# One core of Trainium2: attention values with the attention weights as the stationary operand, and a causal mask made by 64-row products

## The chip, the cores and the metric

The kernel runs on one core of one Trainium2 chip. The metric is the device time in microseconds (us) of one execution. TensorE (PE) does the matrix products and has a second row of records for its weight loads (PEld); VectorE (DVE), ScalarE (ACT) and GpSimd (POOL) do the rest; SyncE (SP) issues most transfers.

## The reference

One layer of an encoder runs for a prompt of 1024 tokens and a sample of 64 tokens. Only the second of its three head groups, the stick-breaking attention with 4 heads of 64, is touched:

```python
def sb_block(q, q_pos, k, v, k_pos):
    z = jnp.einsum('bqhd,bkhd->bhqk', q, k).astype(F32) * (B_HEAD_DIM ** -0.5)
    mask = (k_pos[None, :] < q_pos[:, None])[None, None]
    log_1m = jnp.where(mask, jax.nn.log_sigmoid(-z), 0.0)
    after = lax.cumsum(log_1m, axis=3, reverse=True) - log_1m
    w = jnp.where(mask, jnp.exp(jax.nn.log_sigmoid(z) + after), 0.0)
    return jnp.einsum('bhqk,bkhd->bqhd', w.astype(v.dtype), v)
...
    b_out = o_b.reshape(bsz, L, B_WIDTH) * jax.nn.silu(bg)
```

## The kernel before, in words

The whole layer is one program. Its stages follow each other along the span: norms and memory keys and values, the input projection with the HGRN2 scan beside it (to about 441 us), the attention beside the last projections (about 441 to 577 us), the output projection, cross-attention, and its output projection. Large products are split into three passes of high and low parts (`mm<-hhi,whi`, `mm<-hlo,whi`, `mm<-hhi,wlo`): they are the bulk of PE's work. Here they are called the main products.

The attention is `sb_all`. Two heads form a pair; a pair's keys lie on partitions 0 to 63 for one head and 64 to 127 for the other. A token tile is 128 queries (the ninth is the sample's 64). For each pair and tile there are one or two units, each of at most 512 keys; a tile of two units does the later keys first. That makes 13 units for a pair and 26 in all, of which 18 are a tile's first. A unit passes three steps:

- `scores` (line 629): for each head three products of queries and keys, 64 rows deep, into a bank `hg` each; the two heads' products alternate and use different halves of the array's rows. In a tile's first unit, a product of `identb` (identity) and `negmask` (128 rows deep) then adds -1e30 above the diagonal. ACT makes two sigmoids of each bank, DVE a scan and a product; the result is `sm`, a row for each query.
- `weights_T` (line 658): the weights are transposed on PE in blocks of 128 (`tp<-ident,sm`), and ACT copies them to `wT`, a row for each key.
- `values` (line 677): for each chunk of 128 keys and each head one product with the values `vb` as the stationary operand (128 rows, 64 columns) and `wT` as the moving one (128 queries). The heads fill different halves of the output's partitions. After the tile's last unit DVE multiplies the bank with the gate in `C`.

A product of plain float32 operands leaves two records on PE and two on PEld; a transpose leaves one of each, and so do the main products. The 148 products of values are 296 records.

Two layers set the order. A planner (`Sched`) runs each stage as a task and, at each `yield`, resumes the first task whose inputs it holds ready by its own table of costs; `sb_all` yields once per iteration `k`, which does `scores` of unit k, `values` of unit k-2 and `weights_T` of unit k-1. Then the tile framework orders the instructions of each engine once more by its own model, which can put an instruction of one step inside another. Banks are few: three `hg`, two `tp`, three `mm`.

Of the kernel before, what the change touches and what calls it, by code (L numbers as in the profile page):

```python
# [8 lines left out]
F32 = mybir.dt.float32  # L9
F32R = mybir.dt.float32r  # L10
BF16 = mybir.dt.bfloat16
# [4 lines left out]
P = 128  # L16
# [3 lines left out]
SMP = 64  # L20
# [18 lines left out]
def _rows(i):  # L39
    return P if i < 8 else SMP  # L40
# [64 lines left out]
def hybrid_step(  # L105
# [44 lines left out]
    def ps_tp():  # L150
        return ps.tile([P, 512], F32, tag="tp", name="tp", bufs=2)
# [33 lines left out]
    def tt(out, a, b, op):  # L185
        sch.op("DVE", 0.07 + free(out) / 960.0)
        cur['DVE'] = DVE.tensor_tensor(out=out, in0=a, in1=b, op=op)  # L187
# [20 lines left out]
    with tc.high_priority(offset=10 * URGENT):  # L208
        ones = const([P, P], F32, "ones")
        DVE.memset(ones, 1.0)  # L210
        ident = const([P, P], F32, "ident")
        make_identity(nc, ident)
        mhalf = const([P, 4], F32, "mhalf")
        POOL.memset(mhalf, -0.5)

        identb = const([P, P], BF16, "identb")
        negmask = const([P, P], BF16, "negmask")
        DVE.memset(negmask, 0.0)
        POOL.affine_select(out=negmask, in_=negmask, pattern=[[-1, P]], compare_op=ALU.is_gt,
                           fill=NEG, base=0, channel_multiplier=1)  # L220
        cur["masks"] = (identb, negmask)
        blkmask = const([P, 4], F32, "blkmask")
        DVE.memset(blkmask, 0.0)
        for i in range(4):
            DVE.memset(blkmask[32 * i:32 * i + 32, i:i + 1], 1.0)
        invw = const([P, 2], F32, "invw")
        invcnt = const([P, 2, 16], F32, "invcnt")
        for ct in range(2):
            POOL.iota(invcnt[:, ct, :], pattern=[[1, 16]], base=1, channel_multiplier=0,
                      allow_small_or_imprecise_dtypes=True)  # L230
            for g in range(2):
                w = float(2 << (2 * ct + g))
                rs = slice(64 * g, 64 * g + 64)
                DVE.memset(invw[rs, ct:ct + 1], 1.0 / w)

    def late_constants(pool):
        wpl = pool([P, 2, P], F32, "wpl")
        DVE.memset(wpl, 0.0)
        DVE.tensor_copy(identb, ident)
        for ct in range(2):  # L240
            for g in range(2):
                rs = slice(64 * g, 64 * g + 64)
                DVE.tensor_scalar(out=invcnt[rs, ct, :], in0=invcnt[rs, ct, :], scalar1=float(2 << (2 * ct + g)),
                                  scalar2=None, op0=ALU.min)
        DVE.reciprocal(invcnt, invcnt)
        for g in range(4):
            rs = slice(64 * (g % 2), 64 * (g % 2) + 64)
            POOL.dma_start(wpl[rs, g // 2, rs], w_pool[0, g])
        onorm = const([P, 4], F32, "onorm")
        POOL.dma_start(onorm, hgrn_onorm_g)  # L250
        pscale = const([P, 2], F32, "pscale")
        POOL.dma_start(pscale, pool_scale)
        cur["hgrn"] = (blkmask, onorm)
        cur["pool"] = (invw, invcnt, wpl, pscale)
# [359 lines left out]
    def sb_all(ops, pool):  # L614

        units = []
        for pair in range(2):
            for i in range(NT):
                base, W = (0, P * (i + 1)) if i < 8 else (SEQ, P + SMP)
                nkt = (W + P - 1) // P  # L620
                lo = 0 if W <= 512 else P * (nkt // 2)
                ps_ = [(lo, W)] if lo == 0 else [(lo, W), (0, lo)]
                for pi, (s0, s1) in enumerate(ps_):
                    units.append(dict(pair=pair, i=i, base=base, s0=s0, n=s1 - s0, first=pi == 0,
                                      last=pi == len(ps_) - 1, prev=[None, None]))
        for a, b in zip(units[:-1], units[1:]):
            b["before"] = a

        def scores(u):
            (qh, ql), (kh, kl), vb, cv = ops[u["pair"]]  # L630
            i, n, nq = u["i"], u["n"], _rows(u["i"])
            u["s"], u["m"] = [], []
            zs = [ps_hg(), ps_hg()]
            qs = slice(i * P, i * P + nq)
            ks = slice(u["base"] + u["s0"], u["base"] + u["s0"] + n)
            for pi, (q, k) in enumerate(((qh, kh), (qh, kl), (ql, kh))):
                for e in range(2):
                    own = slice(64 * e, 64 * e + 64)
                    mm(zs[e][:nq, :n], q[own, qs], k[own, ks], pi == 0, pi == 2 and not u["first"])
            if u["first"]:  # L640
                for z in zs:
                    mm(z[:nq, n - nq:n], cur["masks"][0][:nq, :nq], cur["masks"][1][:nq, :nq], False, True)
            for e, z in enumerate(zs):
                s = pool([P, 512], F32, "sm", 7)
                m = pool([P, 512], F32, "sm", 7)
                act(m[:nq, :n], z[:nq, :n], AF.Sigmoid, scale=-0.125)
                act(s[:nq, :n], z[:nq, :n], AF.Sigmoid, scale=0.125)
                p = None if u["first"] else u["before"]["m"][e]
                sch.op("DVE", 0.07 + n / 480.0)
                DVE.tensor_tensor_scan(m[:nq, :n][:, ::-1], m[:nq, :n][:, ::-1], m[:nq, :n][:, ::-1],  # L650
                                       1.0 if p is None else p[:nq, 0:1], ALU.mult, ALU.min)
                if p is not None:
                    tt(s[:nq, n - 1:n], s[:nq, n - 1:n], p[:nq, 0:1], ALU.mult)
                tt(s[:nq, :n - 1], s[:nq, :n - 1], m[:nq, 1:n], ALU.mult)
                u["s"].append(s)
                u["m"].append(m)

        def weights_T(u):
            i, n, nq = u["i"], u["n"], _rows(u["i"])
            npc = (n + P - 1) // P  # L660
            u["wT"] = []
            for e in range(2):
                s = u["s"][e]
                pt = ps_tp()
                wT = pool([P, 4, P], F32, "wT", 4)
                for c in range(npc):
                    w = min(P, n - c * P)
                    tr(pt[:w, c * P:c * P + nq], s[:nq, c * P:c * P + w], nq)
                ptv = pt.rearrange("p (c t) -> p c t", t=P)
                if i < 8:  # L670
                    act(wT[:, :npc, :], ptv[:, :npc, :], AF.Copy)
                else:
                    act(wT[:, 0, :nq], ptv[:, 0, :nq], AF.Copy)
                    act(wT[:SMP, 1, :nq], ptv[:SMP, 1, :nq], AF.Copy)
                u["wT"].append(wT)

        def values(u):
            (qh, ql), (kh, kl), vb, cv = ops[u["pair"]]
            i, n, nq = u["i"], u["n"], _rows(u["i"])
            npc = (n + P - 1) // P  # L680
            po = ps_hg() if u["first"] else u["before"]["po"]
            u["po"] = po
            for c in range(npc):
                for e in range(2):
                    own = slice(64 * e, 64 * e + 64)
                    first, last = u["first"] and c == 0, u["last"] and c == npc - 1
                    if i < 8:
                        mm(po[own, :nq], vb[:, u["s0"] // P + c, own], u["wT"][e][:, c, :], first, last, 0.147)
                    elif c == 0:
                        mm(po[own, :nq], cv[:, own], u["wT"][e][:, 0, :nq], first, last, 0.1)  # L690
                    else:
                        mm(po[own, :nq], vb[:SMP, 8, own], u["wT"][e][:SMP, 1, :nq], first, last, 0.1)
            if u["last"]:
                cs = C[:, i, 4 + u["pair"], :nq]
                tt(cs, po[:, :nq], cs, ALU.mult)
                sch.done[("sb", u["pair"], i)] = sch.t["DVE"]

        nu = len(units)
        for k in range(nu + 2):
            if k < nu:  # L700
                j, c = units[k]["pair"], units[k]["i"] // 3
                if units[k]["first"] and (k == 0 or units[k]["i"] % 3 == 0 or c == 2):
                    yield f"bv{j}{c}"
                ready = dict(sch.cur.dep)
                scores(units[k])
            if 0 <= k - 2 < nu:
                values(units[k - 2])
            if 0 <= k - 1 < nu:
                weights_T(units[k - 1])
            yield None  # L710


# [747 lines left out]
```

## Time and profile before

| | |
|---|---|
| median of 3 runs | 935.03 us (934.71 to 935.86) |
| the profiled execution | 935.02 us; its span 933.3 us, granted clock 0.996 |
| PE busy in the span | 914.2 us (98%) |
| PEld, DVE, ACT, POOL busy | 853.6, 556.6, 479.5, 107.2 us |

Busy time of PE is the union of its records. A record lasts some 270 ns although the next can start 110 ns after it, so how long a stretch of products takes is read from the starts of its first and of the next group. "Idle before" is what no record covers, and the releaser behind the arrow is what ended it. In a timeline the columns are the start, the time covered, and the group with its count.

### The profile page before, as it was taken

The numbers are of one execution on the slowest core, as the hardware profiler recorded it, in microseconds if no ns is written. First come the engines' busy times: TensorE is split into PE (matmuls) and PEld (weight loads), VectorE is DVE, ScalarE is ACT, GpSimd is POOL, SyncE is SP. The second block draws the span as 40 slices with busy tenths as digits, with TensorE's granted clock in tenths as the row PEclk, the third lists the DMA queues.
The fourth block names the chain that finished last, engine by engine and source line by source line (L and its number), as shares of the span: only waits on it lengthen the run. The fifth ranks groups of instructions, "written<-read, shape, count | busy, mean of one in ns | idle before, by whom it ended". The sixth has DMA issues, their size and how long they took to land.

```text
span 933.3 us, 18372 instructions
## 1 busy us (share of the span) xinstructions
PE 914.2 (98%) x7504; PEld 853.6 (91%) x7504; DVE 556.6 (60%) x1125; ACT 479.5 (51%) x1005; POOL 107.2 (11%) x194
## 2 busy tenths in 40 slices
PE   8899999999999999999999999999999999999997
PEld 7899999999998999989779788999999999999997
DVE  6849483674678574552684777565564545563343
ACT  7623384658767774963673765433452333342231
POOL 5502430010010010000000000211200000001110
PEclk9999999999999999999999999999999999999999
DMA  8815511011100111012111411222433111232231
GB/s 306 259 38 181 142 46 47 25 49 29 47 27 31 47 33 46 25 47 79 47 31 36 157 61 69 90 68 80 164 119 92 30 39 46 76 106 91 91 101 58
DMA packets 33126, 73.60 MB, mean 79 GB/s; under 512 B 5601, under 2 KB 18065, under 8 KB 33042
## 3 DMA queue, kind: packets, MB, share of 16 engines
q1 hardware_dynamic: 30112, 68.07, 22.7%
q0 software_dynamic: 1888, 4.35, 1.3%
q8 instruction: 59, 0.97, 0.4%
q14 instruction: 25, 0.20, 0.1%
q10 hardware_dynamic: 1042, 0.01, 0.1%
HBM read 56.45 MB, written 15.89 MB: 78 GB/s over the span
## 4 chain that ended last, share of the span: by engine, by line
PE 82%; DVE 6%; ACT 4%; DMA 4%; issue 2%; POOL 1%; DVEq 0%; POOLq 0%; ACTq 0%
PE mm L171 64%; PE hg L171 14%; PE tp L175 5%; DVE sm L650 3%; DVE sm L187 1%; DVE wlo L187 1%; ACT L183 1%; ACT whi L183 1%; DMA xt<-in_x_prompt_dram 1%; DVE hlo L187 1%; DMA wraw<-in_w_xk_dram 1%; DMA mkd<-mraw 1%; DMA wraw<-in_w_xo_dram 1%; DMA gT<-in_norm_mem_dram 1%; DMA mvd<-mtm 1%
## 5 line engine op out<-in xcount | busy, mean ns | idle before, releaser
L171 PE MATMUL mm<-hhi,whi 128*128 128x384 f32 (+2 forms) x1272 | 425.1, 334 | 0.0
L171 PE MATMUL mm<-hlo,whi 128*128 128x384 f32 (+2 forms) x1272 | 412.5, 325 | 0.0
L171 PE MATMUL mm<-hhi,wlo 128*128 128x384 f32 (+2 forms) x1248 | 405.3, 325 | 0.0
L171 PEld LDWEIGHTS mm<-hhi,whi 128*128 128x128 f32 x1272 | 239.2, 188 | 6.3 <-issue 1.3
L171 PEld LDWEIGHTS mm<-hlo,whi 128*128 128x128 f32 x1272 | 239.5, 188 | 1.2 <-issue 0.9
L171 PEld LDWEIGHTS mm<-hhi,wlo 128*128 128x128 f32 x1248 | 234.6, 188 | 0.4 <-issue 0.3
L187 DVE TENSOR_TENSOR wlo<-wraw,whi 128x1024 fp32r<-128x1024 f32 (+1 forms) x53 | 63.5, 1200 | 56.6 <-ACT whi L183 56.3
L183 ACT ACT_TABLE_LOAD x66 | 84.7, 1283 | 19.0 <-DVE E L187 12.0
L183 ACT ACTIVATE whi<-wraw 128x1024 fp32r<-128x1024 f32 (+1 forms) x53 | 55.3, 1043 | 71.5 <-PE mm L171 54.7
L183 ACT ACTIVATE wraw<-mm 128x384 f32<-128x384 f32 (+3 forms) x51 | 22.9, 449 | 72.8 <-PE mm L171 62.9
L650 DVE TENSOR_TENSOR_SCAN sm<-sm 128x384 f32<-128x384 f32 (+4 forms) x52 | 48.3, 938 | 14.0 <-ACT sm L183 14.0
L183 ACT ACTIVATE sm<-hg 128x384 f32<-128x384 f32 (+4 forms) x104 | 42.2, 485 | 15.7 <-PE hg L171 8.7
L187 DVE TENSOR_TENSOR wraw<-mm,gain 128x384 f32<-128x384 f32 (+1 forms) x48 | 24.4, 510 | 41.6 <-ACT wraw L183 41.3
L1241 POOL TENSOR_TENSOR small<-small 128x1 f32<-128x1 f32 (+1 forms) x18 | 4.2, 234 | 375.3 <-ACT wraw L183 375.3
L183 ACT ACTIVATE E<-E 128x512 f32<-128x512 f32 (+1 forms) x68 | 32.8, 515 | 10.5 <-DVE E L187 9.9
L171 PE MATMUL mm<-mhi,wlo 128*128 128x256 f32 x128 | 35.8, 289 | 1.8 <-DVE wlo L187 1.8
L321 POOL TENSOR_TENSOR small<-small,mhalf 128x1 f32<-128x1 f32 (+2 forms) x50 | 36.0, 719 | 4.2
L171 PE MATMUL mm<-mhi,whi 128*128 128x256 f32 x128 | 36.2, 293 | 0.1
L171 PE MATMUL mm<-mlo,whi 128*128 128x256 f32 x128 | 35.1, 283 | 0.0
L443 POOL COPY qf<-q 128x512 f32<-128x512 f32 (+1 forms) x12 | 14.6, 1218 | 177.6 <-PE hg L171 140.7
L187 DVE TENSOR_TENSOR wlo<-C,whi 128x1024 fp32r<-128x1024 f32 x16 | 19.6, 1225 | 24.9 <-ACT whi L183 23.4
L191 DVE SCALAR_TENSOR_TENSOR C<-wraw,small,C 128x384 f32<-128x384 f32 (+3 forms) x54 | 27.8, 569 | 10.2 <-POOL small L321 10.2
(209 smaller groups left out, 1409.1 us busy)
## 6 DMA issues: line engine op xcount, KB each, us to landing
wraw<-in_w_in_dram SPq DMA_DIRECT2D x28, 512.0 KB, 3.6
xt<-in_x_prompt_dram SPq DMA_DIRECT2D x8, 512.0 KB, 6.5
wraw<-in_w_xv_dram SPq DMA_DIRECT2D x8, 512.0 KB, 3.9
wraw<-in_w_out_dram SPq DMA_DIRECT2D x8, 512.0 KB, 3.6
C<-in_x_prompt_dram SPq DMA_DIRECT2D x8, 512.0 KB, 3.5
x1d<-C SPq DMA_DIRECT2D x8, 512.0 KB, 2.8
wraw<-in_w_xq_dram SPq DMA_DIRECT2D x8, 512.0 KB, 3.6
wraw<-in_w_xo_dram SPq DMA_DIRECT2D x8, 512.0 KB, 3.6
```

The source lines that it names most:

```text
L171: cur['PE'] = PE.matmul(out, lhsT=lhsT, rhs=rhs, start=start, stop=stop, skip_group_check=True)
L175: PE.transpose(out, in_, ident[:n, :n])
L183: cur['ACT'] = ACT.activation(out, in_, func, **kw)
L187: cur['DVE'] = DVE.tensor_tensor(out=out, in0=a, in1=b, op=op)
L191: DVE.scalar_tensor_tensor(out=out, in0=a, scalar=s, in1=b, op0=op0, op1=op1)
L321: POOL.tensor_tensor(out=r[:n, :w], in0=r[:n, :w], in1=mhalf[:n, :w], op=ALU.pow)
L443: POOL.tensor_copy(qf[:, 1, :], qq)
L650: DVE.tensor_tensor_scan(m[:nq, :n][:, ::-1], m[:nq, :n][:, ::-1], m[:nq, :n][:, ::-1], 1.0 if p is None else p[:nq, 0:1], ALU.mult, ALU.min)
L1241: POOL.tensor_tensor(out=ms[:n, 0:1], in0=ms[:n, 0:1], in1=ms[:n, pi:pi + 1], op=ALU.add)
```

## The change

The values' product changes sides: `wT` (128 queries wide) becomes the stationary operand and `vb` (64 columns of one head) the moving one. The output has a row for each query; the heads lie side by side in columns of the bank. The first and the second unit of a tile write different 128 columns, since each closes its own sum. After the tile's last unit ACT copies the bank to `vo`, DVE adds the second half where there is one, and a new step `gated`, one iteration later, transposes `vo` on PE and multiplies with the gate. The iteration now does `scores` of unit k, `weights_T` of k-1, `gated` of k-3, `values` of k-2. The mask is made of products 64 rows deep and 64 columns wide: `picks` holds identity blocks for each half of the rows, and two products for each head replace the one. The planner's cost of a product of values goes from 0.147 (0.1 for the sample's) to 0.113.

```diff
-        identb = const([P, P], BF16, "identb")
-        negmask = const([P, P], BF16, "negmask")
+        picks = const([P, 2, P], BF16, "picks")
+        negmask = const([P, 64], BF16, "negmask")
...
+        for e in range(2):
+            POOL.affine_select(out=negmask[64 * e:64 * e + 64], in_=negmask[64 * e:64 * e + 64], pattern=[[-1, 64]],
+                               compare_op=ALU.is_gt, fill=NEG, base=0, channel_multiplier=1)
...
-        DVE.tensor_copy(identb, ident)
+        DVE.memset(picks, 0.0)
+        for e in range(2):
+            es = slice(64 * e, 64 * e + 64)
+            for i in range(2):
+                DVE.tensor_copy(picks[es, i, 64 * i:64 * i + 64], ident[es, es])
+            DVE.memset(picks[64 * e:64 * e + 1, 1, 0:64], 1.0)
...
             if u["first"]:
-                for z in zs:
-                    mm(z[:nq, n - nq:n], cur["masks"][0][:nq, :nq], cur["masks"][1][:nq, :nq], False, True)
+                picks, negmask = cur["masks"]
+                for hf in range(nq // 64):
+                    for e in range(2):
+                        own = slice(64 * e, 64 * e + 64)
+                        c0 = n - nq + 64 * hf
+                        mm(zs[e][:nq, c0:c0 + 64], picks[own, hf, :nq], negmask[own], False, hf == nq // 64 - 1)
...
-            for c in range(npc):
-                for e in range(2):
-                    own = slice(64 * e, 64 * e + 64)
-                    first, last = u["first"] and c == 0, u["last"] and c == npc - 1
-                    if i < 8:
-                        mm(po[own, :nq], vb[:, u["s0"] // P + c, own], u["wT"][e][:, c, :], first, last, 0.147)
...
+            c0 = 0 if u["first"] else P
+            for e in range(2):
+                own = slice(64 * e, 64 * e + 64)
+                for c in range(npc):
+                    kn = SMP if i == 8 and c else P
+                    v = cv if i == 8 and c == 0 else vb[:, 8 if i == 8 else u["s0"] // P + c]
+                    mm(po[:nq, c0 + 64 * e:c0 + 64 * e + 64], u["wT"][e][:kn, c, :nq], v[:kn, own], c == 0, c == npc - 1,
+                       0.113)
             if u["last"]:
+                vo = pool([P, P], F32, "vo", 1)
+                act(vo[:nq], po[:nq, :P], AF.Copy)
+                if c0:
+                    tt(vo[:nq], po[:nq, P:2 * P], vo[:nq], ALU.add)
+                u["vo"] = vo
+
+        def gated(u):
+            i, nq = u["i"], _rows(u["i"])
+            if u["last"]:
+                pt = ps_tp()
+                tr(pt[:, :nq], u["vo"][:nq], nq)
                 cs = C[:, i, 4 + u["pair"], :nq]
-                tt(cs, po[:, :nq], cs, ALU.mult)
+                tt(cs, pt[:, :nq], cs, ALU.mult)
...
+            if 0 <= k - 1 < nu:
+                weights_T(units[k - 1])
+            if 0 <= k - 3 < nu:
+                gated(units[k - 3])
             if 0 <= k - 2 < nu:
                 values(units[k - 2])
-            if 0 <= k - 1 < nu:
-                weights_T(units[k - 1])
```

The order of PE's instructions in the two programs shows what becomes of a unit. (A product's two records are one row here; the size is that of its output.) This is the first unit of the last prompt tile of the second pair before: scores and mask, then the values of the unit two before it, then the transposes of the one just before it.

```order
L171 MATMUL hg<-kh,qh 128x512 x2
L171 MATMUL hg<-kl,qh 128x512 x2
L171 MATMUL hg<-kh,ql 128x512 x2
L171 LDWEIGHTS identb
L171 MATMUL hg<-negmask,identb 128x128
L171 LDWEIGHTS identb
L171 MATMUL hg<-negmask,identb 128x128
L171 MATMUL hg<-wT,vb 64x128 x8
L175 MATMUL tp<-ident,sm 128x128 x6
```

The same place on PE after the change, from the last of the four mask products on, with the tile's second unit behind it:

```order
L171 MATMUL hg<-negmask,picks 128x64
L175 MATMUL tp<-ident,sm 128x128 x6
L171 MATMUL hg<-vb,wT 128x64 x8
L171 MATMUL hg<-kh,qh 128x512
L171 MATMUL hg<-kl,qh 128x512
L171 MATMUL hg<-kh,qh 128x512
L171 MATMUL hg<-kl,qh 128x512
L175 MATMUL tp<-ident,vo 128x128
L171 MATMUL hg<-kh,ql 128x512 x2
L175 MATMUL tp<-ident,sm 128x128 x8
L171 MATMUL hg<-vb,wT 128x64 x6
```

The transposes have moved ahead of the values, and the mask is four products. In the second unit, whose scores stood two by two before, the two heads' products no longer all alternate, and the transpose of `vo` stands among them.

More of the change, by code (lines that the diff above doesn't have):

```diff
@@ L214, in hybrid_step @@
         POOL.memset(mhalf, -0.5)
-        identb = const([P, P], BF16, "identb")
-        negmask = const([P, P], BF16, "negmask")
+        picks = const([P, 2, P], BF16, "picks")
+        negmask = const([P, 64], BF16, "negmask")
         DVE.memset(negmask, 0.0)
-        POOL.affine_select(out=negmask, in_=negmask, pattern=[[-1, P]], compare_op=ALU.is_gt,
-                           fill=NEG, base=0, channel_multiplier=1)
-        cur["masks"] = (identb, negmask)
+        for e in range(2):
+            POOL.affine_select(out=negmask[64 * e:64 * e + 64], in_=negmask[64 * e:64 * e + 64], pattern=[[-1, 64]],
+                               compare_op=ALU.is_gt, fill=NEG, base=0, channel_multiplier=1)
+        cur["masks"] = (picks, negmask)
         blkmask = const([P, 4], F32, "blkmask")
@@ L682, in values @@
             u["po"] = po
-            for c in range(npc):
-                for e in range(2):
-                    own = slice(64 * e, 64 * e + 64)
-                    first, last = u["first"] and c == 0, u["last"] and c == npc - 1
-                    if i < 8:
-                        mm(po[own, :nq], vb[:, u["s0"] // P + c, own], u["wT"][e][:, c, :], first, last, 0.147)
[L689 to L692, printed above, removed]
-            if u["last"]:
+            c0 = 0 if u["first"] else P
[6 more added lines that the diff above has]
+                       0.113)
+            if u["last"]:
+                vo = pool([P, P], F32, "vo", 1)
[8 more added lines that the diff above has]
+                tr(pt[:, :nq], u["vo"][:nq], nq)
                 cs = C[:, i, 4 + u["pair"], :nq]
-                tt(cs, po[:, :nq], cs, ALU.mult)
+                tt(cs, pt[:, :nq], cs, ALU.mult)
                 sch.done[("sb", u["pair"], i)] = sch.t["DVE"]
         nu = len(units)
-        for k in range(nu + 2):
+        for k in range(nu + 3):
             if k < nu:
```

## The prediction

> **What bounds the kernel now.** I read the page's totals first, then the stage of the attention in a table by stretches, then PE's timeline inside that stage, and last the list of waits.
>
> ```profile
> PE 914.2 (98%) x7504; PEld 853.6 (91%) x7504; DVE 556.6 (60%) x1125; ACT 479.5 (51%) x1005; POOL 107.2 (11%) x194
> PE 82%; DVE 6%; ACT 4%; DMA 4%; issue 2%; POOL 1%; DVEq 0%; POOLq 0%; ACTq 0%
> core 0: us, PE busy (x) PEld busy (x) DVE busy (x) ACT busy (x) POOL busy (x), PEclk, DMA share, GB/s
> 441.00:577.00 136.00, 132.16 (x1044) 108.96 (x1043) 96.40 (x164) 88.35 (x209) 0.20 (x1) 1.00 0.19 59
> ```
>
> The second line is the chain that ended last by engine. PE bounds the whole program, and in the attention's stage it leaves only 136.00 - 132.16 = 3.84 us uncovered, while DVE and ACT have 39 us and more to spare. The clock is full. So a product added to PE here lengthens the span, unless it falls into those 3.84 us; a product's price is the distance to the start of the next one.
>
> The timeline of PE, last prompt tile of the second pair (start, time covered, group, count):
>
> ```profile
> 561.73 0.50 PE L171 MATMUL hg<-kh,qh 64*128 64x512 f32 x2
> 562.06 0.40 PE L171 MATMUL hg<-kl,qh 64*128 64x512 f32 x2
> 562.29 0.40 PE L171 MATMUL hg<-kh,ql 64*128 64x512 f32 x2
> 562.63 0.29 PE L171 MATMUL hg<-negmask,identb 128*128 128x128 bf16 x2
> 562.84 1.09 PE L171 MATMUL hg<-wT,vb 128*64 128x128 f32 x16
> 563.87 0.87 PE L175 MATMUL tp<-ident,sm 128*128 128x128 f32 x6
> 564.50 0.37 PE L171 MATMUL mm<-hhi,whi 128*128 128x256 f32 x1
> ...
> 565.70 0.39 PE L171 MATMUL hg<-kl,qh 64*128 64x512 f32 x2
> 565.93 0.40 PE L171 MATMUL hg<-kh,ql 64*128 64x512 f32 x2
> 566.26 0.88 PE L171 MATMUL hg<-wT,vb 128*64 128x128 f32 x12
> 567.07 1.27 PE L175 MATMUL tp<-ident,sm 128*128 128x128 f32 x8
> ```
>
> Sixteen records of values take 563.87 - 562.84 = 1.03 us to the next group, twelve take 567.07 - 566.26 = 0.81: 0.055 us for each further record and 0.15 per block. The form 128*64 says that a record uses half of the array's columns; the two heads run side by side, so one head's record lasts 0.11 and two share it.
>
> Changes of the form cost. From one score pass to the next are 562.29 - 562.06 = 0.23 us, but from the last pass to the mask 0.34 and to the values 0.33: 0.11 and 0.10 more. The 0.15 per block of values is of this kind too (its end into the transposes).
>
> **The values.** The new form, 128 rows by 128 stationary columns with 64 moving ones, both float32, stands once in this trace: cross-attention's sample product, stationary `cvm`. First its groups beside those of the values now, then its place in PE's and PEld's timelines.
>
> ```profile
> L171 PE MATMUL hg<-wT,vb 128*64 128x128 f32 x288 | 22.0, 281 | 1.5 <-DVE C L187 0.9 <-ACT wT L183 0.5
> L171 PE MATMUL hg<-PTs,cvm 128*128 128x64 f32 x32 | 4.4, 261 | 0.0
> L171 PEld LDWEIGHTS hg<-PTs,cvm 128*128 128x128 f32 x32 | 4.3, 192 | 0.0
> 715.67 0.56 PE L171 MATMUL hg<-PTs,cvm 128*128 128x64 f32 x4
> 716.03 0.36 PE L171 MATMUL hg<-PTh,Vh 128*128 128x256 f32 x1
> 716.24 0.28 PE L171 MATMUL hg<-PTl,Vh 128*128 128x256 f32 x1
> 716.35 0.28 PE L171 MATMUL hg<-PTh,Vl 128*128 128x256 f32 x1
> 715.55 0.54 PEld L171 LDWEIGHTS hg<-PTs,cvm 128*128 128x128 f32 x4
> 716.01 0.19 PEld L171 LDWEIGHTS hg<-PTh,Vh 128*128 128x128 f32 x1
> ```
>
> Four weight loads take 716.01 - 715.55 = 0.46 us, 0.115 each. On PE the four records take 0.36 and the product behind them is late by another 0.10 (0.21 to its successor, where the next one needs 0.11): 0.115 again. Idle before is 0.0: nothing waits, the loads of 128 columns follow each other and set the pace, although 64 moving columns would need half of 0.11. I take 0.112 a record; the heads no longer share, since both outputs fill all 128 partitions.
>
> Before, 296 x 0.055 = 16.3 us without the block ends. After, 288 x 0.112 = 32.3, and the sample's 8 records (64 stationary columns) about 0.06 each, 0.5: 32.8. **+16.5 us**, all on PE.
>
> A rule speaks against the change. The Trainium skill ("TensorEngine Tiling (Array Packing)", When to Use Tiling) advises, for a moving side of at most 64 columns, to swap the operands and tile the columns, up to twice as fast: that is the form before. By it a record would go from 0.055 to at most 0.11, +15.8 us here. The rows above say 0.112 and go slightly beyond its limit.
>
> **Changes of form.** Removed: the block ends 26 x 0.15 = 3.9, the entries to the values 26 x 0.10 = 2.6, the entry to the mask 18 x 0.11 = 2.0. Added: from the 64-row products straight to the transposes, 26 x 0.11 = 2.9 (same step as into the mask). The values then follow transposes of their own form at no cost. Sum **-5.6 us**.
>
> **The mask.** 36 products of 128 columns become 68 of 64, two of which can run side by side in different halves of the rows. Two before took 562.84 - 562.63 = 0.21 with the step behind them. I take no difference; 36 x 0.03 = 1 us either way is its bound.
>
> **`vo` and its transpose.** 18 transposes on PE at 0.63 / 6 = 0.105 (row of 563.87): **+2.0 us**. The 18 copies on ACT and 8 additions on DVE are priced by
>
> ```profile
> L183 ACT ACTIVATE sm<-hg 128x128 f32<-128x128 f32 x8 | 1.6, 283 | 0.8 <-PE hg L171 0.8
> L187 DVE TENSOR_TENSOR C<-hg,C 128x128 f32<-128x128 f32 x16 | 4.6, 285 | 1.0 <-PE hg L171 1.0
> ```
>
> at 18 x 0.28 = 5.1 and 8 x 0.285 = 2.3 us; both engines have over 39 us free in the stage, so PE hides them. Were it idle, each copy with its addition would be some 0.6 us on the path. Behind `vo` on ACT stand the next unit's sigmoids.
>
> **The order.** In PE's order after the change, 9 of the 18 `vo` transposes stand between score products, and 52 score products stand alone where 18 did (the others in pairs). The price of both is seen where the order before already did this:
>
> ```profile
> 524.22 0.33 PE L171 MATMUL hg<-kl,qh 64*128 64x384 f32 x1
> 524.39 0.34 PE L171 MATMUL hg<-kh,ql 64*128 64x384 f32 x1
> 526.15 0.50 PE L171 MATMUL hg<-kh,qh 64*128 64x512 f32 x1
> 526.58 0.65 PE L175 MATMUL tp<-ident,sm 128*128 128x128 f32 x4
> 527.17 0.50 PE L171 MATMUL hg<-kl,qh 64*128 64x512 f32 x1
> ```
>
> A score product alone takes 0.17 (384 keys) to 0.23 (512), as long as a pair. 34 more alone are 17 more passes of about 0.2: +3.4. A transpose between scores costs 0.43 - 0.33 = 0.10 going in and 0.59 - 4 x 0.105 = 0.17 coming out: 9 x 0.27 = +2.4. Together **+5.8 us**, with 0 (the heads overlap after all) and 8 as ends.
>
> **Waits.** The largest waits of PE in the stage, and one that PEld shows without a releaser, the changes of form:
>
> ```profile
> PE tp L175 <- DVE sm L187: 2.3, 3, 1.3
> PEld hg L171 <- ACT wT L183: 2.8, 11, 0.4
> PEld hg L171 <- issue: 5.6, 25, 0.4
> ```
>
> The transposes now come before the values, hence earlier after the scores; behind a waiting transpose stand the values and the next main products. But each iteration has more PE work, which covers the sigmoids and the scan of the unit before better. Of the 3.84 us uncovered I take back 2: **-2 us**; ends -4 (all of it) and +4 (18 waits of 0.2 for the copy to `vo` or for one of two `tp` banks).
>
> At the start DVE prepares `picks` with seven instructions where one did, and the norm's transposes stand elsewhere in PE's order. PE waits there as well as DVE; I take 0, with 2 us either way.
>
> **Sum**: 16.5 - 5.6 + 2.0 + 5.8 - 2 = +16.7 on the profiled execution's 935.02, which is the median (935.03) within 0.01: **952 us**, a span of about 950, an attention stage of about 153 instead of 136. The ends: 16.5 - 5.6 + 2.0 + 0 - 4 - 2 = +7, 942; 16.5 - 5.6 + 2.0 + 8 + 4 + 2 = +27, 962.
>
> **Rivals.**
> 1. The weight loads hide (other side). If the next weights load while a product runs, a record needs only its 64 moving columns, half of 0.11 = 0.055. Then 288 x 0.057 = 16.4 us less: +0.3, or -1.7 if all idle time goes: **934 us**, not slower. It decides from about 0.055 a record; at 0.06 the kernel is already slower by 2. Against it: the loads of `cvm` 0.115 apart with no idle before them. This is also what the Trainium skill says ("TensorE: Matmul & The Clock Gate", Step-by-step): the next tile's weights load during this tile's product. The rows of `cvm` show that the loads do run beside the products, and yet pace them when they are the longer of the two.
> 2. PE has slack. The chain of waits gives PE 82%, and 6% to DVE; were the stage paced by sigmoid, scan and product, added PE work would partly vanish. For it: the wait of 1.3 above. Against: 3.84 us uncovered is all there is. With the order's costs hidden in waits as well (-5.8, and -4 instead of -2): **944 us**.
> 3. `vo` becomes the wait. `po` is freed by a copy on ACT in place of a product on DVE, behind two copies to `wT`, and `gated` needs a third `tp` bank of two. If each of 18 transposes waits 0.6 us (copy and addition), +10.8 in place of -2: **965 us**.
>
> **How the numbers follow.** Forecast (944 to 960) 0.70; rival 2 0.10; rival 3 0.12; rival 1 0.06, split evenly between same and faster; 0.02 for weight loads that hide in part and a start that gains besides, split likewise. The runs spread by about 0.1%, so 0.2% (1.9 us) is what a measurement can tell from no change. Slower 0.92, same 0.04, faster 0.04. The range 942 to 962 leaves out rival 1, those 0.02 and half of rival 3: 0.14.
>
> **What would show it.** PE's record of `hg<-vb,wT` comes 288 times in form 128*128 128x64; four in a row take 0.45 us, and a block of 16 about 1.8 to the next group. No jump stands before transposes or main products behind values; the idle of PEld put to "issue" shrinks. PE stays over 96% busy from 441 to about 594. If 16 records take 0.9, rival 1 holds; if PE waits before `tp<-ident,vo` for ACT, rival 3; if the stage's idle was far more than 3.84, rival 2.

## The result and the profile after

| | before | after |
|---|---|---|
| median | 935.44 us (934.71 to 935.88) | **947.9 us** (947.44 to 951.21) |
| ratio, 95% interval | | 1.0142 [1.0117, 1.0166] |
| the profiled execution, its span | 935.02, 933.3 us | 951.21, 949.5 us |

The change makes the kernel 12.5 us slower by the medians; the interval of the ratio is 10.9 to 15.5 us. The forecast was 952 us (942 to 962).

The page's totals and the chain that ended last, by engine:

```profile
PE 930.6 (98%) x7554; PEld 875.9 (92%) x7554; DVE 560.3 (59%) x1139; ACT 483.8 (51%) x1023; POOL 106.1 (11%) x195
PE 86%; DVE 4%; ACT 4%; DMA 3%; issue 1%; POOL 1%; DVEq 0%; POOLq 0%; ACTq 0%
```

PE's busy time grew by 16.4 us, its share of the chain from 82% to 86%. By stretches, with the columns as before: the attention's stage of after, the rest of after, and the rest of before.

```profile
443.00:591.00 148.00, 145.96 (x1077) 128.07 (x1076) 98.49 (x171) 90.41 (x223) 0.19 (x1) 1.00 0.17 54
591.00:944.00 353.00, 351.47 (x2292) 345.13 (x2292) 183.54 (x373) 125.43 (x315) 34.37 (x69) 1.00 0.26 86
577.00:928.00 351.00, 349.11 (x2277) 342.23 (x2275) 182.93 (x372) 123.63 (x313) 35.04 (x70) 1.00 0.26 86
```

The stage, with its edges set at whole microseconds, took 136.00 us and now takes 148.00, of which 2.04 (148.00 - 145.96) are uncovered where 3.84 were. The rest is 2 us longer and has 15 more records (x2292 after, x2277 before), main products that have moved out of the stage. The clock is full in both.

The groups of PE, PEld and ACT that are new (busy, mean ns of one, idle before):

```profile
L171 PE MATMUL hg<-vb,wT 128*128 128x64 f32 x288 | 36.6, 270 | 0.0
L171 PEld LDWEIGHTS hg<-vb,wT 128*128 128x128 f32 x288 | 35.0, 192 | 0.8 <-issue 0.6
L175 PE MATMUL tp<-ident,vo 128*128 128x128 f32 x16 | 5.0, 312 | 0.0
L183 ACT ACTIVATE vo<-hg 128x128 f32<-128x128 f32 x16 | 4.6, 286 | 6.4 <-PE hg L171 4.3 <-PE tp L175 2.0
```

PE's timeline in the second pair's last prompt tiles: a block of twelve, and behind it a block of sixteen with the second unit that The change lists:

```profile
565.17 0.39 PE L171 MATMUL hg<-kh,ql 64*128 64x512 f32 x2
565.40 0.23 PE L171 MATMUL hg<-negmask,picks 64*128 64x64 bf16 x4
565.57 0.87 PE L175 MATMUL tp<-ident,sm 128*128 128x128 f32 x6
566.28 1.45 PE L171 MATMUL hg<-vb,wT 128*128 128x64 f32 x12
567.66 0.44 PE L171 MATMUL hg<-kh,qh 64*128 64x384 f32 x1
...
574.79 1.90 PE L171 MATMUL hg<-vb,wT 128*128 128x64 f32 x16
576.61 0.50 PE L171 MATMUL hg<-kh,qh 64*128 64x512 f32 x2
576.95 0.40 PE L171 MATMUL hg<-kl,qh 64*128 64x512 f32 x2
577.28 0.33 PE L175 MATMUL tp<-ident,vo 128*128 128x128 f32 x1
577.54 0.50 PE L171 MATMUL hg<-kh,ql 64*128 64x512 f32 x2
577.97 0.66 PE L175 MATMUL tp<-ident,sm 128*128 128x128 f32 x4
579.01 0.66 PE L175 MATMUL tp<-ident,sm 128*128 128x128 f32 x4 [0.39 <-DVE C L187]
579.51 1.45 PE L171 MATMUL hg<-vb,wT 128*128 128x64 f32 x12
580.77 0.42 PE L171 MATMUL mm<-hhi,whi 128*128 128x384 f32 x1
```

Sixteen records of values take 576.61 - 574.79 = 1.82 us to the scores, twelve 567.66 - 566.28 = 1.38: 0.11 a record, twice the 0.055 of before. The last score pass steps to the mask in 0.23 us, as to another pass (0.34 before).

The waits in the stage (total us, times, longest):

```profile
PE tp L175 <- DVE C L187: 0.8, 2, 0.4
PE tp L175 <- ACT vo L183: 0.7, 1, 0.7
PE tp L175 <- DVE sm L187: 0.5, 2, 0.4
PEld hg L171 <- issue: 4.5, 21, 0.2
PEld tp L175 <- DVE C L187: 1.5, 3, 0.6
```

The wait of the transposes for DVE's scan and product (`sm`) fell from 2.3 to 0.5, and the new ones are small.

To compare kernels, all of PE's time from the first score product to its last record is divided up in each profiled execution: the distance from each record to the start of the next goes to the first one's group. "Rest" holds all other products to the end of the program; "uncovered" is what no record covers in that time, and is inside the other columns (a wait stands in the step of the record ahead of it). The start is left out because its length varies by itself: the first score product came between 439.9 and 444.2 us in these profiles, at 441.59 before and 443.32 after.

| us | scores | mask | tp sm | values | tp vo | rest | sum | uncovered |
|---|---|---|---|---|---|---|---|---|
| before | 20.9 | 6.3 | 18.3 | 21.5 | 0 | 418.3 | 485.3 | 4.9 |
| after | 21.2 | 4.4 | 19.7 | 33.8 | 3.7 | 417.1 | 499.8 | 2.9 |
| values_only | 24.2 | 3.1 | 19.1 | 33.5 | 3.7 | 417.1 | 500.7 | 3.2 |
| mask_only | 19.2 | 7.3 | 18.6 | 21.5 | 0 | 419.1 | 485.6 | 6.0 |
| tiled_late | 22.3 | 4.9 | 24.7 | 23.7 | 0 | 418.3 | 493.8 | 6.8 |
| order_back | 19.5 | 4.9 | 15.6 | 34.1 | 3.0 | 418.4 | 495.5 | 2.6 |
| own_bank | 18.7 | 4.4 | 21.9 | 35.1 | 2.4 | 417.2 | 499.6 | 6.8 |
| wide_moving | 19.9 | 4.2 | 22.8 | 37.2 | 3.7 | 416.8 | 504.6 | 6.5 |
| halves | 22.3 | 4.5 | 23.9 | 27.2 | 4.2 | 417.9 | 499.9 | 5.2 |
| one_load | 23.8 | 4.8 | 21.3 | 23.4 | 3.8 | 421.4 | 498.5 | 7.7 |

After against before: values +12.3, their transposes +3.7, transposes of `sm` +1.4, scores +0.3, mask -1.9, rest -1.3: +14.4. The medians differ by 12.5; the profiled execution of after was the slowest of its four, with a gap of 2.9 us on PE in the start.

### The profile page after: what moved, and what is told of

It reads as the page before. It is cut to its first block, busy times and chain, and to the rows that moved or that the text cites. A ratio compares the mean times of both kernels' runs of the same rounds, so it can differ in the third digit from the quotient of the medians.

```text
span 949.5 us, 18498 instructions
## 1 busy us (share of the span) xinstructions
PE 930.6 (98%) x7554; PEld 875.9 (92%) x7554; DVE 560.3 (59%) x1139; ACT 483.8 (51%) x1023; POOL 106.1 (11%) x195
## 3 DMA queue, kind: packets, MB, share of 16 engines
q1 hardware_dynamic: 30112, 68.07, 22.3%
## 4 chain that ended last, share of the span: by engine, by line
PE 86%; DVE 4%; ACT 4%; DMA 3%; issue 1%; POOL 1%; DVEq 0%; POOLq 0%; ACTq 0%
PE mm L171 64%; PE hg L171 17%; PE tp L175 5%; DVE sm L662 1%; ACT L183 1%; DVE sm L187 1%; DMA xt<-in_x_prompt_dram 1%; DVE wlo L187 1%; ACT whi L183 1%; DMA wraw<-in_w_xv_dram 0%; DMA mkd<-mraw 0%; DMA mvd<-mtm 0%; DMA xt<-in_mem_prompt_dram 0%; POOL small L329 0%; ACT junk L183 0%
## 5 line engine op out<-in xcount | busy, mean ns | idle before, releaser
L183 ACT ACTIVATE wraw<-mm 128x384 f32<-128x384 f32 (+3 forms) x51 | 22.8, 448 | 72.4 <-PE mm L171 62.5
L171 PE MATMUL hg<-vb,wT 128*128 128x64 f32 (+1 forms) x296 | 37.9, 270 | 0.0
L187 DVE TENSOR_TENSOR hlo<-tp,hhi 128x512 fp32r<-128x512 f32 (+1 forms) x36 | 22.5, 656 | 24.8 <-ACT hhi L183 24.8
L171 PEld LDWEIGHTS hg<-vb,wT 128*128 128x128 f32 (+1 forms) x296 | 35.8, 190 | 1.1 <-issue 0.6
```

The source lines that it names most:

```text
L171: cur['PE'] = PE.matmul(out, lhsT=lhsT, rhs=rhs, start=start, stop=stop, skip_group_check=True)
L183: cur['ACT'] = ACT.activation(out, in_, func, **kw)
```

## The experiments

**The parts alone.** `values_only` has the new values, transposes and order with the mask of before; `mask_only` the 64-row mask with the values and the order of before.

```diff
 mask_only, against after (values_only keeps these lines, and takes back picks and negmask)
-                    mm(po[:nq, c0 + 64 * e:c0 + 64 * e + 64], u["wT"][e][:kn, c, :nq], v[:kn, own], c == 0, c == npc - 1,
-                       0.113)
+                    if i < 8:
+                        mm(po[own, :nq], vb[:, u["s0"] // P + c, own], u["wT"][e][:, c, :], first, last, 0.147)
```

> Only the values are changed (wT stationary, vo and its transpose, the order of the steps); the mask is one product of 128 rows as before, and the program's start keeps the order of before. Theory: the changed kernel plus the 18 steps into the mask, about 2 to 3 us more from the first score product to the end (16 to 17 us over before): 950 to 953 us. Rival (values and mask each cost half): 941 us.

> Only the mask is changed: four products 64 rows deep, values and their place as before. Theory (each change of TensorE's form costs about 0.1 us; the weight loads make the values dear): 18 steps from scores to mask go, 18 x 0.11 = 2.0 us, and the mask's products cost no more; 932 to 934 us against 935.4. Rival (the mask is where the change loses): 940 us or more. The start of the program has the order of the changed kernel, so up to 2 us either way come with it; the time from the first score product to the end tells the two apart.

`values_only`: 949.9 us, ratio 1.0163 [1.0135, 1.019]; from the first score product on it takes 0.9 us more than after where 2 to 3 were expected. `mask_only`: 935.45 us, 1.0006 [0.9992, 1.0021], no difference: the 932 to 934 of its theory did not come. Yet PE has less to do there. Its timeline, at the place shown of before:

```profile
561.55 0.40 PE L171 MATMUL hg<-kh,ql 64*128 64x512 f32 x2
561.79 0.23 PE L171 MATMUL hg<-negmask,picks 64*128 64x64 bf16 x4
561.95 1.09 PE L171 MATMUL hg<-wT,vb 128*64 128x128 f32 x16
```

From the last score pass to the values are 0.24 + 0.16 = 0.40 us, where before had 0.34 + 0.21 = 0.55: 0.15 less. But where main products follow the mask, the step out of the 64-row form takes the gain back, and the waits grow (that for `sm` was 2.3 before):

```profile
PE tp L175 <- DVE sm L187: 2.7, 4, 1.4
PE hg L171 <- DVE C L187: 1.1, 1, 1.1
```

Scores and mask together save 0.8 us in the table, and uncovered time rises by 1.1. So the whole loss is in the values and the order, and PE work that is removed need not shorten this stage (here it didn't).

**What paces a record.** `wide_moving` gives each product 128 moving columns (its own 64 twice, of which one copy is used); `halves` cuts each product into two of 64 stationary columns that write different halves of the output's partitions.

```diff
 wide_moving
+                    mm(po[:nq, c0 + P * e:c0 + P * e + P].rearrange("p (r t) -> p r t", t=64), u["wT"][e][:kn, c, :nq],
+                       v[:kn, own].unsqueeze(1).broadcast_to([kn, 2, 64]), c == 0, c == npc - 1, 0.113)
 halves
+                    for r in range(nq // 64):
+                        rs = slice(64 * r, 64 * r + 64)
+                        mm(po[rs, c0 + 64 * e:c0 + 64 * e + 64], u["wT"][e][:kn, c, rs], v[:kn, own], c == 0,
+                           c == npc - 1, 0.056)
```

> The changed kernel with 128 moving columns in place of 64 in each product of values (the head's 64 columns twice; one of the two copies is dropped when the bank is copied to vo). Theory (the loads of 128 stationary columns set the pace): a record stays at 0.11 us and the time at that of the changed kernel, 945 to 949 us; the order has fewer score products alone (20 for 52), worth up to 3 us less. Rival (the moving columns set it): a record goes to about 0.22 or at least by half, 288 x 0.055 to 0.11 = 16 to 32 us more, 964 to 980 us.

> The changed kernel with each product of values cut into two of 64 queries: 64 stationary columns, 64 moving, outputs on different halves of the partitions, so two could run side by side. Theory A (loads go one after the other, whatever half of the array they fill, and their columns are all that counts): as many columns as in the changed kernel, so 0.11 us for each pair of records and the time of the changed kernel, plus changes of form before and after the values as in the old kernel, 26 x 0.15 to 0.25 = 4 to 6 us: 951 to 955 us. Theory B (loads into different halves overlap): half the time for the values, 288 x 0.055 = 16 us less, plus the changes of form: 935 to 938 us.

`wide_moving`: 953.28 us, 1.0191 [1.0169, 1.0213]. Its group, and a block of twelve:

```profile
L171 PE MATMUL hg<-vb,wT 128*128 128x128 f32 x288 | 37.5, 276 | 0.0
580.67 1.50 PE L171 MATMUL hg<-vb,wT 128*128 128x128 f32 x12
581.93 0.42 PE L171 MATMUL mm<-hhi,whi 128*128 128x384 f32 x1
```

Twelve records take 581.93 - 580.67 = 1.26 us to the main products, as in after (580.77 - 579.51). Twice the moving columns cost nothing in a record: the loads of 128 columns set the pace, and rival 1 falls. The kernel is slower all the same, above the 945 to 949 us of its theory and far below the 964 of the rival; of the 4.8 us over after that the table shows, 3.6 are uncovered time.

`halves`: 949.8 us, 1.0157 [1.0133, 1.0181]. Two blocks of its values:

```profile
568.29 0.92 PE L171 MATMUL hg<-vb,wT 128*64 128x64 f32 x24
569.14 0.44 PE L171 MATMUL hg<-kh,qh 64*128 64x384 f32 x1
...
576.60 1.15 PE L171 MATMUL hg<-vb,wT 128*64 128x64 f32 x32
577.68 0.83 PE L171 MATMUL hg<-kh,qh 64*128 64x512 f32 x2
```

Eight more records take 1.08 - 0.85 = 0.23 us more, 0.029 each and 0.058 for two that fill both halves, where one whole record took 0.11: loads into different halves go side by side. It also shows that 0.11 is no fixed price of a record: a load of half the columns takes half of it. The values fall by 6.6 us, but the form 128*64 brings the steps at a block's entry and exit back (transposes of `sm` +4.2, scores +1.1), and uncovered time rises by 2.3: nothing is left. The time lies below theory A (951 to 955 us) and far above theory B (935 to 938), although in these blocks two records came at theory B's price.

**The order.** `order_back` has the new values with the parts of an iteration in the order of before; `tiled_late` the old values (and the 64-row mask) with the transposes ahead of them.

```diff
 order_back, against after (tiled_late moves weights_T the other way in mask_only)
-            if 0 <= k - 1 < nu:
-                weights_T(units[k - 1])
             if 0 <= k - 3 < nu:
                 gated(units[k - 3])
             if 0 <= k - 2 < nu:
                 values(units[k - 2])
+            if 0 <= k - 1 < nu:
+                weights_T(units[k - 1])
```

> The changed kernel with the iteration's steps in the old order (scores of unit k, gated of k-3, values of k-2, transposes of k-1). In PE's order no transpose of vo stands between scores (9 did) and 30 score products stand alone (52 did). Theory (PE's own time decides, the order's prices as predicted: 9 x 0.27 and 11 passes of 0.2): 4.6 us less than the changed kernel, 943 us. Rival (the mask alone removed 2.3 us of PE time and the stage kept its length, since waits for sigmoids, scan and copies took it back: the stage is held by that chain as well): 946 to 948 us.

> The kernel before with the 64-row mask and the new place of the transposes (ahead of the values, behind the scores), values still in the old form: the order alone. 50 score products stand alone instead of 18, 16 passes more; changes of form in all 117 instead of 90. Theory A (work added to PE counts in full, as the prediction priced it): 16 x 0.2 = 3.2 us and 14 more pairs of changes of form, of 0.1 in and 0.15 out, 3.4 us: 941 to 942 us. Theory B (the earlier transposes feed the values earlier and the waits of PE, 5 us, pay for it): within 1 us of 935.

`order_back`: 946.67 us (943.95 to 947.11), 1.0106 [1.0085, 1.0128]. `tiled_late`: 943.26 us, 1.0096 [1.0078, 1.0114], 7.8 us over `mask_only`. With the sums of the table the four kernels form a square: the new order adds 8.2 us to the old values (485.6 to 493.8) and 4.3 to the new ones (495.5 to 499.8); the new values add 9.9 in the old order and 6.0 in the new. The order alone is a loss, in PE's own work: uncovered time grows by only 0.8 and 0.3 us. In `tiled_late` 50 score products stand alone in the program where 18 did, and the scores take 3.1 us more (theory A: 3.2); the whole is a little over theory A's 941 to 942 us, and theory B (935) falls.

```profile
563.10 0.44 PE L171 MATMUL hg<-kh,qh 64*128 64x384 f32 x1
563.38 0.33 PE L171 MATMUL hg<-kl,qh 64*128 64x384 f32 x1
563.56 0.34 PE L171 MATMUL hg<-kh,ql 64*128 64x384 f32 x1
...
PE tp L175 <- DVE sm L187: 4.7, 6, 1.4
```

The last line is of its list of waits: the transposes, now right behind the scores, wait 4.7 us for the scan's product, where after waits 0.5. Two things make values and order cost less together than one by one. The old values behind the transposes pay a change of form going in and coming out (values +2.2 us with the order, of which 1.2 are uncovered), the new ones don't (-0.3). And the new values, being longer, cover waits: uncovered time falls with them from 6.0 to 2.6 us in the old order and from 6.8 to 2.9 in the new. In the new form the traces side with the theory of `order_back` (4.3 us, expected 4.6), its median with the rival (946 to 948): the medians differ by 1.2 us, the ratios by 0.36%, which is 3.4 us, and their intervals overlap. How much of the 4.3 the median would keep is open.

**The bank.** `own_bank` takes the transpose of `vo` from the main products' three banks instead of the transposes' two. That also moves it on PE: none stands among scores (9 did), and 34 score products stand alone (52 did).

```diff
 own_bank: gated(u)
-                pt = ps_tp()
+                pt = ps_mm()
```

> The changed kernel with one edit: the transpose of the finished values takes one of the three banks of the main products in place of one of the two banks of the transposes. With that bank free, the order of PE changes too: none of the 18 transposes of the values stands between score products (9 did), 34 score products stand alone (52 did), and changes between the scores' form and the full form fall from 38 each way to 29. Theory A (the prediction's prices hold for the order): 9 x 0.27 = 2.4 us less for the transposes among scores, 18 single products fewer are 9 passes of 0.2 = 1.8 us less, and the wait of the transposes for the gated product on DVE (2.3 us of PE's and PEld's waits) goes: about 5 us less in the stage, 943 us. Theory B (work taken off PE comes back as waits for sigmoid, scan and copies, as it did when the old order was put back): at most 1.5 us less, 946.5 us, with larger waits of the transposes of sm for DVE and ACT. Rival 3 of the prediction (the two banks are the wait) gives 4 us or more.

949.14 us, 1.0159 [1.0136, 1.0182]: theory B, without even its 1.5 us. The table tells why. Scores fall by 2.5 us and the transposes of `vo` by 1.2, together 3.7 where theory A priced 4.2; uncovered time rises by 3.8. The waits of PE for `C` are gone and others have come:

```profile
PE tp L175 <- ACT sm L183: 2.9, 4, 1.2
PE tp L175 <- ACT vo L183: 1.2, 1, 1.2
PE hg L171 <- ACT sm L183: 1.1, 1, 1.1
```

The first is the sigmoid. With nothing left between scores and transposes, what was a wait for a bank is, by these releasers, a wait for the unit's own chain. The bank comes out of the main products' three, so what a third one added to the transposes' two would do was not run.

**One load a product.** `one_load` rounds the values' operands (`wT`, `vb`, `cv`) to float32r, in PE's order of after: one record and one load a product. The rounded values are also the ones handed out. `one_load_back` adds the old order, `one_load_bank` and `one_load_back_bank` the bank of `own_bank` to either.

```diff
-                wT = pool([P, 4, P], F32, "wT", 4)
+                wT = pool([P, 4, P], F32R, "wT", 4)
...
-            vb = pool([P, NT, P], F32, "vb", 2)
+            vb = pool([P, NT, P], F32R, "vb", 2)
```

> The changed kernel, same order on PE, with wT and the values rounded to the one-pass float32 that the split products use (the values handed out are rounded too): each product of values leaves one record and one weight load in place of two. Theory (a load of 128 columns costs 0.11 us on PE and all of it counts): blocks of values go from 33.8 to about 17.9 us, and the time from 947.9 to 932. Rival (the chain of sigmoid, scan and copies holds the stage): blocks as low, but a third or more of it comes back as waits of PE in the attention, 937 to 942 us.

> Both together: one load for each product of values (rounded as in the run with one load), and the steps in the old order. Theory (sums on PE): 932 - 4.6 = 927 to 928 us, below the kernel before. Rival (the chain holds the stage at the length it has in the kernel before, about 134 us): 934 to 937 us, no better than the kernel before.

> The changed kernel with the values' operands rounded to float32r (one weight load a product; the values handed out are rounded with them), and with the bank of the transpose of the values taken from the main products, as in the kernel own_bank, in the same order of PE. The one-load kernel without that bank lost its 16 us of loads to waits and a lower clock and took 947.2. Theory A (the wait for the transposes' banks, 3.5 us on PE and 5.3 on PEld for DVE's gated product, held the stage, and everything else followed): 935 us or less, the waits named DVE C near 0 and the granted clock back at 0.996 or above. Theory B (the chain of score, sigmoid, scan, transpose, copy and values of one unit after the other holds the stage, whatever the bank): 941 to 946, with the waits now named sm, wT and vo. Theory C (the lower clock is the cause, and comes with the form of the products): the clock stays at 0.990 and the time within 2 us of 947.

> The same rounding and the same bank, with the order of before for the parts of an iteration (scores, gated product, values, transposes of the next unit). 8 score products stand alone, 74 in pairs (30 and 63 with the transposes' bank), and 28 changes of form each way. Theory A: PE's own work in the stage is some 16 us less than in the changed kernel with its order put back (946.7), of which the bank lets pass 12 to 14: 933 us, at or below the kernel before, spread as narrow as that kernel's. Theory B (unit chain): 937 to 942, as the one-load kernel with the old order (median 942.4). If the granted clock of single runs falls below 0.99 again, those runs are 5 us and more slower than the others.

| | median (runs) | ratio to before | clock of the runs |
|---|---|---|---|
| one_load | 947.22 us (943.87 to 947.98) | 1.0116 [1.0096, 1.0137] | 0.989 to 0.992 |
| one_load_bank | 944.69 us (943.97 to 948.55) | 1.0113 [1.0093, 1.0134] | 0.988 to 0.993 |
| one_load_back | 942.4 us (936.06 to 945.35) | 1.0059 [1.0037, 1.0081] | 0.988 to 0.996 |
| one_load_back_bank | 940.01 us (936.82 to 944.66) | 1.0053 [1.0032, 1.0073] | 0.989 to 0.995 |

152 records of 0.11 less are 16.7 us of PE work, and `one_load` gains 0.7 by the medians: neither its theory (932 us) nor its rival (937 to 942) came, nor did those of `one_load_back` (927 to 928, 934 to 937). Two things ate the gain. Uncovered time is 4.7 us more than in after, with the transposes' wait for `C` the largest. The other is the clock, by stretches of 10 us (the granted clock stands behind POOL's count); the last row is of its list of waits:

```profile
530.00:540.00 10.00, 8.88 (x61) 6.97 (x60) 9.79 (x17) 8.38 (x23) 0.00 (x0) 0.94 0.22 65
540.00:550.00 10.00, 10.00 (x61) 8.66 (x60) 7.55 (x16) 7.27 (x20) 0.00 (x0) 0.72 0.21 69
...
570.00:580.00 10.00, 8.06 (x59) 6.14 (x58) 8.90 (x17) 7.16 (x21) 0.19 (x1) 0.99 0.01 2
580.00:590.00 10.00, 10.00 (x42) 9.24 (x43) 1.43 (x4) 1.99 (x6) 0.11 (x1) 0.50 0.16 52
...
PE tp L175 <- DVE C L187: 3.5, 7, 0.7
```

What the clock took of these four is, as an estimate, 10 us times its missing share: 0.6 + 2.8 + 0.1 + 5.0 = 8.5 us. With the 4.7 and the gain of 1.2 in the table's sum that is 14.4 of the 16.7; the rest is open. Theory A of `one_load_bank` falls too: without the transposes' bank the wait for `C` is gone, but 6.2 us now wait for `sm`, as theory B had it, and the clock still falls, in the profiled run to 0.993. `one_load_back_bank` lies in its theory B (937 to 942). None of the four beats the kernel before; `one_load_back` reaches 936.06 in its one run with a clock of 0.996.

## Why the prediction was right

**The bound.** "So a product added to PE here lengthens the span": it did. The stage grew by 12.0 us, and its uncovered time fell by 1.8, for which the prediction took back 2.

**The values**, +16.5, with the block ends of -3.9: 12.6. Measured 33.8 - 21.5 = 12.3. The price of a record, 0.112 from four records of `cvm`, is 0.11 in the blocks of 12 and 16, and `wide_moving` shows the reason given for it. The Trainium skill ("TensorEngine Tiling (Array Packing)", Key Properties) says that different tiles load weights and multiply in parallel; `halves` agrees, with two records in 0.058 us. By the Trainium skill's advice on the swap (the same page, When to Use Tiling) the old form was the better one, and so the kernel's time says.

**The other changes of form and the mask.** The entry to the mask is gone (0.34 to 0.23), and from mask to transposes are 0.17 us where the two products of before took 0.21 to the values. The table's -1.9 for the mask is uncovered time (2.7 us stood in its steps before, 0.7 after); its own work is the same, as predicted. And `mask_only` shows that the entries to the mask (-2.0 of the -5.6) brought the old form nothing.

**`vo`.** 2.0 for the transposes and 9 x 0.17 for leaving them among scores is 3.5; measured 3.7.

**The order**, +5.8, is the term that was mis-sized, in the number of its passes. The prediction counted lone score products in the program's order: 52 where 18 stood, 17 passes more. On the chip fewer ran alone. At 576.61 above, the second unit's first four stand singly in the program (they are listed in The change: `kh,qh` and `kl,qh` of one head, then of the other), yet they start two by two, at 576.61 and 576.95, and are done in 0.67 us, the step into `vo` included; four passes of 0.23 alone would be 0.92. Before had this too, with products that stand singly in the program as well. The prediction's last row of that place is a `kl,qh` of one head at 527.17; the rows behind it are:

```profile
527.17 0.50 PE L171 MATMUL hg<-kh,qh 64*128 64x512 f32 x1
527.50 0.39 PE L171 MATMUL hg<-kh,ql 64*128 64x512 f32 x1
527.51 0.39 PE L171 MATMUL hg<-kl,qh 64*128 64x512 f32 x1
```

Each starts with one of the other head: 527.17 with 527.17, 527.50 with 527.51. So what the prediction set as the low end of this term, that the heads overlap after all, is in part what happened. Counted by starts less than 60 ns apart, 95 passes ran where before has 86: 9 more (7 if 120 ns are allowed) and not 17, which makes the term 9 x 0.2 + 2.4 = 4.2. The scores' column bears it out: with the prediction's other terms in it (-2.0 for the entries to the mask, 0.1 for the 8 units without one, +0.9 for nine entries to `vo`) 9 passes give +0.8 and 17 give +2.4; it grew by 0.3.

The runs do not test each price by itself. `tiled_late` paid 3.1 us in the scores (priced 3.2), and `own_bank` got 3.7 of PE's steps back (priced 4.2), but had 3.8 more uncovered. `order_back`, which leaves 30 lone products in the program, was priced at 4.6 below after and is 4.3 below by the traces; but scores have only 1.7 of this, and transposes of `sm` 4.1 with -1.4 in the rest.

**The start**, 0 with 2 either way: +1.7 in the profiled execution (443.32 against 441.59), within the spread of the starts here (439.9 to 444.2).

**The sum**, +16.7, against +14.4 in the traces and 12.5 in the medians. The 8 passes that did not come are 1.6 of the 2.3 us between forecast and traces. For the transposes of `sm` (+1.4) and the rest (-1.3) the prediction had nothing; that they cancel is luck. The 1.9 between traces and medians, in which the start has its part, were not settled; the traces' 14.4 lies within the interval of 10.9 to 15.5.

**The rivals.** Rival 1 falls with `wide_moving`. Rival 3 falls with after itself: the waits that bear on it are 0.8 and 0.7 us on PE and 1.5 on PEld, where it asked for 10.8; and another bank for `vo` brings no gain (`own_bank`). Rival 2, that PE has slack, is half right. It fails for work added, since the values' 12.3 us are there in full. For work removed it holds in `mask_only` and `own_bank`, and beside the clock in `one_load`: there waits on score, sigmoid, scan and transpose of a unit came up in place of the work. It does not hold for what `order_back` removed, whose uncovered time is no larger (2.6 us, after 2.9). That the chain of a unit was nearly full as well is read from these waits; no run changes the chain alone.

## What to carry to other kernels

Price a small product by the longer of two times, its load's and its moving side's, and count what runs beside it: here turning the operands made two loads that lay side by side into one that fills the array, and every record twice as long. Where an engine is 98% busy, added work counted in full here, but removed work must be checked against the chain of the other engines before it is called a gain. Count what runs alone in a trace and not in the program: products that stand singly there can start in pairs. When a change carries an order with it, time the order alone: by the traces it cost 8 us in the old form and 4 in the new.

## What was not expected of the hardware

In `one_load` the granted clock fell to 0.50 for a stretch of 10 us behind one in which records covered 8.06 of 10 us and no gap was longer than 0.73 (the rows of 570 to 580 and 580 to 590 above). The Trainium skill ("TensorE: Matmul & The Clock Gate", Why this matters for your kernels) names idle gaps of more than about 3 us as what throttles the clock; no gap of PE in the stage of `one_load` is longer than 0.97 us, so that sentence does not account for this fall. Short gaps alone don't either. `own_bank`, with float32 values, had a stretch nearly as thin at the full clock, with a wait of 1.21 us in it:

```profile
530.00:540.00 10.00, 8.32 (x70) 6.61 (x69) 9.61 (x15) 8.75 (x21) 0.00 (x0) 1.00 0.54 167
```

Of the profiled executions only those of the four kernels with rounded values lost clock in this stage, and their runs vary by up to 9 us. What in them sets it off was not settled.
